# A one-core diffusion block: handovers between layers issued from a build-time plan, and token blocks turned in pairs by a product with diag(scale)

## The chip, the cores and the metric

The kernel runs on one core of one Trainium2 chip. The metric is the device time of one execution in microseconds (us). The engines are named as in the profile: PE is the matrix engine (PEld its weight loads), DVE the vector engine, ACT the scalar engine, POOL the GpSimd engine, SP the engine that issues most DMAs. Each engine runs its own instructions in the order in which they stand in its queue; a wait for another engine is a semaphore.

## The reference, cut to what matters

The program is a two-layer backbone on 512 latent tokens and 256 context tokens of width 1024. Each layer has a token mixer (layer 0 retention, layer 1 HGRN2) and a ConvGLU channel mixer, so there are four sub-layers. Between two sub-layers stands the same piece of arithmetic, and the change is made there:

```python
def rms_norm(x, g):
    y = xf * lax.rsqrt(jnp.mean(xf * xf, -1, keepdims=True) + NORM_EPS)
    return (y * g.astype(jnp.float32)).astype(x.dtype)
...
        h_l = h_l + g1_l * rms_norm(y_l, norm_g[i, 1])
        u_l = rms_norm(h_l, norm_g[i, 2]) * (1.0 + sc2_l) + sh2_l
        h_l = h_l + g2_l * rms_norm(conv_ffn(u_l, ...), norm_g[i, 3])
```

A sub-layer's output y is normalised over the 1024 features of each token, scaled and added to the stream h; h is normalised again and modulated, which gives the next sub-layer's input u. Everything is float32.

## The kernel before

**Arithmetic of the products.** Float32 operands are split into a high and a low part (`split`: an ACT copy makes the high part, a DVE or POOL subtraction the low one), and a product is three matmuls on the parts (`mm3`). Matmuls on operands that were not split, plain float32, are few; each appears in the trace as two rows of PE. A transpose through PE appears as one.

**A handover.** There are four: `m0` after retention and `e0` after the first ConvGLU, on 768 tokens (6 blocks of 128), `m1` after HGRN2 and `e1` after the last ConvGLU, on 512 tokens (4 blocks). In each, `tail` runs the last quarter of the output projection: per block b and half c of the 1024 columns, 12 matmuls into one PSUM bank named `tl`. The order is block by block, the last two blocks interleaved. In the first banks (two, in `m1` four) the last three matmuls are held back. There are six banks of the kind `mm`, which `tl` and `ld` share, and two small ones, used for turned blocks.

**One block after its two banks** (`handover`, generator `block`): DVE adds the bank to y (L375), ACT squares it with a running sum (L376), twice; DVE adds the sums (L377); `rstd` takes ACT for the root (L98) and three short DVE steps (L99 to L101); DVE scales y (L379) and adds it to h (L380); POOL sends h to DRAM (L385); ACT squares h (L386); `rstd` again; ACT writes h times the factor (L389). Then the block is turned from tokens x features to features x tokens: eight transposes on PE against an identity (L396) into two small banks, eight ACT instructions of 128 columns that scale and shift (L399), and the split into the four tiles of u (L56, L57). In `e1` there is no next sub-layer, and SP sends h out (L382).

**After the tail** the next sub-layer's first weights (`lead`, two sets of 256 columns, `fl` or `hl`) are split, the first set's low part on POOL, and `lead` runs their products, 24 matmuls of 256 tokens each into banks named `ld`: per pair of blocks four pieces in `m0`, four or two in `e0`, four in `m1`. A pair must be turned before its pieces run. The turns of the later blocks stand between these pieces (`hooks`).

**What sets the order.** PE's order is written out by hand: each turn stands where `next(gens[b])` is called. The orders of DVE, ACT, POOL and SP come from the framework's scheduler at build time.

Of the kernel before, what the change touches and what calls it, by code (L numbers as in the profile page):

```python
# [15 lines left out]
P = 128  # L16
D = 1024
NF = 8
# [11 lines left out]
LATENT = BOTH[:2]  # L30


class Net:
# [61 lines left out]

    def rstd(self, r, w, ssum, n):
        nc = self.nc
        nc.scalar.activation(r, ssum, AF.Abs_reciprocal_sqrt, bias=self.eps, scale=1.0 / n)  # L98
        nc.vector.tensor_tensor(w, r, r, ALU.mult)  # L99
        nc.vector.scalar_tensor_tensor(w, ssum, n * EPS, w, ALU.add, ALU.mult)  # L100
        nc.vector.scalar_tensor_tensor(r, w, -3.0 * n, r, ALU.add, ALU.mult)  # L101
        return r
# [246 lines left out]
    def handover(self, nm, y, hsrc, gain, mods, u, hdst, nb, big, tmp):  # L349
# [7 lines left out]
        small = lambda n, w: self.cp.tile([P, w], F32, tag=f"sm{w}", name=f"{n}{nm}", bufs=6)  # L357

        def load():
            rows = hsrc.rearrange("(b p) d -> p b d", p=P)  # L360
            for j, x in enumerate(hx):
                n = min(3, nb - 3 * j)
                nc.sync.dma_start(x[:, :n], rows[:, 3 * j : 3 * j + n])
            for v in range(g.shape[1]):
                nc.scalar.dma_start(g[:, v], self.gains[gain][v : v + 1].broadcast_to([P, D]))

        def block(b):
            ts, v = slice(b * P, b * P + P), int(b >= 4)
            yb, hb = y[b // per][:, b % per], hx[b // 3][:, b % 3]
            ss = small(f"ss{b}", 4)  # L370
            r = small(f"r{b}", 2)
            for c in range(2):
                cs = slice(c * 512, c * 512 + 512)
                ps = yield
                nc.vector.tensor_tensor(yb[:, cs], ps, yb[:, cs], ALU.add)  # L375
                nc.scalar.activation(tmp(f"sq{nm}{b}{c}"), yb[:, cs], AF.Square, accum_out=ss[:, c : c + 1])  # L376
            nc.vector.tensor_tensor(ss[:, 2:3], ss[:, 0:1], ss[:, 1:2], ALU.add)  # L377
            ry = self.rstd(r[:, 0:1], r[:, 1:2], ss[:, 2:3], D)
            nc.vector.scalar_tensor_tensor(yb, yb, ry, g[:, v], ALU.mult, ALU.mult)  # L379
            nc.vector.tensor_tensor(hb, hb, yb, ALU.add)  # L380
# [8 lines left out]
            nc.scalar.activation(yb, hb, AF.Copy, scale=rh)  # L389
            yield "z"  # L390
            A, B = mods()
            z = yb.rearrange("p (f c) -> p f c", c=P)
            for j in range(2):
                ps = self.sml(f"tr{nm}{b}{j}")
                for f in range(4):
                    nc.tensor.transpose(ps[:, f * P : f * P + P], z[:, 4 * j + f], self.ident)  # L396
                for f in range(4):
                    k = 4 * j + f
                    nc.scalar.activation(z[:, k], ps[:, f * P : f * P + P], AF.Identity,  # L399
                                         scale=A[:, k, v : v + 1], bias=B[:, k, v : v + 1])  # L400
# [24 lines left out]
    def tail(self, w, x, y, nb, mk, nxt, mid=None):  # L425
        load, gens = mk(nb)
        load()
        for g in gens:
            next(g)

        def part(b, c, kr, ps):
            for k in kr:
                xh, xl = (z[:, b * P : b * P + P] for z in x(k))
                for z, (l, r) in enumerate(((xh, w[c][0]), (xh, w[c][1]), (xl, w[c][0]))):
                    self.nc.tensor.matmul(ps, l, r[:, k], start=(k == 0 and z == 0), stop=(k == 3 and z == 2))  # L435
            if kr[-1] == 3:
                gens[b].send(ps)
# [3 lines left out]
        pss = [self.acc(f"tl{self.uid()}") for _ in range(n0)]  # L441
        for e, ps in zip(order, pss):
            part(*e, range(3), ps)
        if mid is not None:
            self.filler(mid)
        for e, ps in zip(order, pss):
            part(*e, range(3, 4), ps)
        done = 0
        for n, (b, c) in enumerate(order[n0:], n0):
            part(b, c, range(4), self.acc(f"tl{self.uid()}"))  # L450
            if nxt and n >= 6 and n % 2 == 0 and done < nb - 3:
                next(gens[done])
                done += 1
        if not nxt:
            return None
        load, ctx = nxt[0]()
        ws = [z() for z in load]
        turn = lambda b: lambda: next(gens[b])
        if nb == 6:
            hooks = {(0, 0): turn(3), (0, 2): turn(4), (1, 0): turn(5)}  # L460
        else:
            turn(1)()
            hooks = {(0, 0): turn(2), (0, 1): turn(3)}
        return self.lead(ws, ctx, nxt[1](), BOTH if nb == 6 else LATENT, hooks)

# [4 lines left out]
    def lead(self, ws, ctx, u, chunks, hooks):  # L470
        pl = [self.acc(f"ld{self.uid()}") for _ in range(4)]
        pc = [None] * 4
        self.lead_ps = pl, pc
        for z in range(2):
            if ctx[z]:
                bank = self.acc(f"ld{self.uid()}")
                pc[2 * z], pc[2 * z + 1] = bank[:, :TC], bank[:, TC : 2 * TC]
        for ci, (t0, v) in enumerate(chunks):
            for j in range(4):
                if v and pc[j] is None:  # L480
                    continue
# [3 lines left out]
                cs = slice(t0, t0 + W)  # L485
                self.mm3([(o, cs)], [(wh[:, k, ms], wl[:, k, ms], *self.uhl(u, k)) for k in range(NF)])
                if (ci, j) in hooks:
                    hooks[ci, j]()
        return [[(pl[j], LAT)] + ([(pc[j], CTX)] if pc[j] is not None else []) for j in range(4)]

    def first(self, u, big, tmp, extra, epi):
# [94 lines left out]
        self.lead(ws, (True, True), u, BOTH, hooks)  # L586
# [284 lines left out]
    def ffn_lead(self, i):  # L871
        wu = self.t["ffn_w_up"][i].rearrange("(k p) n -> p k n", p=P)

        def load(c):
            return self.weights(wu[:, :, c : c + 256], NF, 256, f"fl{i}{c}", None if c else self.nc.gpsimd)

        return [lambda: load(0), lambda: load(FT * P)], (i == 0, i == 0)
# [437 lines left out]
```

## Time and profile before

| what | value |
|---|---|
| time, median of 3 runs (lowest to highest) | 2200.57 us (2200.57 to 2201.64) |
| the profiled execution's own time | 2201.44 us |
| its span in the profile | 2199.7 us |
| mean granted PE clock | 0.985 of full speed |
| instructions | 30760 |
| HBM read and written | 200.90 MB and 15.34 MB |

The span runs from the first to the last instruction of the trace. Within it the handovers begin at 687.2 (`m0`), 1274.1 (`e0`), 1776.4 (`m1`) and 2167.3 us (`e1`), each counted from its first `tl` matmul. A row of a timeline has a start, a duration, the engine, the line of the kernel, the operation, the tiles out<-in, their shape and a count; in brackets stands how long the engine was idle before it and what ended that. The durations of PE rows overlap, since matmuls are pipelined: what a matmul takes of PE is read from one start to the next.

### The profile page before, as it was taken

The numbers are of one execution on the slowest core, as the hardware profiler recorded it, in microseconds if no ns is written. First come the engines' busy times: TensorE is split into PE (matmuls) and PEld (weight loads), VectorE is DVE, ScalarE is ACT, GpSimd is POOL, SyncE is SP. The second block draws the span as 40 slices with busy tenths as digits, with TensorE's granted clock in tenths as the row PEclk, the third lists the DMA queues.
The fourth block names the chain that finished last, engine by engine and source line by source line (L and its number), as shares of the span: only waits on it lengthen the run. The fifth ranks groups of instructions, "written<-read, shape, count | busy, mean of one in ns | idle before, by whom it ended". The sixth has DMA issues, their size and how long they took to land. (4 is left out here: it accounts for less than half of the span.)

```text
span 2199.7 us, 30760 instructions
## 1 busy us (share of the span) xinstructions
PE 2113.7 (96%) x12288; PEld 1779.3 (81%) x12288; DVE 1340.3 (61%) x2500; ACT 864.3 (39%) x1695; POOL 323.0 (15%) x395
## 2 busy tenths in 40 slices
PE   7999999999899899999999999999999879999998
PEld 5888888888788788788888878888888658888886
DVE  6867565663613567477577566777777754434445
ACT  5543333423524633322132176434443445333323
POOL 4622040210100100000000013333333320000000
PEclk9999999999999999999999999999999999999999
DMA  8113313233123233333333422111111242232232
GB/s 293 51 65 98 111 51 125 78 125 125 39 88 132 69 116 106 112 110 126 124 98 133 174 92 90 59 39 58 39 58 39 77 164 101 93 115 83 92 109 109
DMA packets 186030, 218.21 MB, mean 99 GB/s; under 512 B 6048, under 2 KB 157600, under 8 KB 185120
## 3 DMA queue, kind: packets, MB, share of 16 engines
q1 hardware_dynamic: 179856, 198.90, 27.3%
q0 software_dynamic: 2736, 13.11, 1.6%
q10 hardware_dynamic: 3296, 4.26, 0.6%
q8 instruction: 96, 1.57, 0.3%
q14 instruction: 46, 0.38, 0.1%
HBM read 200.90 MB, written 15.34 MB: 98 GB/s over the span
## 5 line engine op out<-in xcount | busy, mean ns | idle before, releaser
L84 PE MATMUL f<-um,hua 128*128 128x512 f32 (+1 forms) x960 | 258.2, 356 | 0.0
L84 PE MATMUL f<-um,huv 128*128 128x512 f32 (+1 forms) x960 | 255.9, 354 | 0.0
L221 DVE SCALAR_TENSOR_TENSOR rows<-rada,sc,rows 128x256 f32<-128x256 f32 x504 | 231.5, 484 | 5.4
L937 PE MATMUL f<-hd,gt 128*128 128x512 f32 x720 | 228.2, 396 | 0.0
L84 PEld LDWEIGHTS f<-um,hua 128*128 128x128 f32 x960 | 169.6, 189 | 29.3 <-issue 4.0
L84 PE MATMUL hp<-ue,hhw 128*128 128x512 f32 (+1 forms) x672 | 192.0, 373 | 0.0
L84 PEld LDWEIGHTS f<-um,huv 128*128 128x128 f32 x960 | 170.0, 189 | 25.3
L84 PE MATMUL f<-um,lua 128*128 128x512 f32 (+1 forms) x480 | 170.1, 354 | 0.0
L84 PE MATMUL f<-um,luv 128*128 128x512 f32 (+1 forms) x480 | 169.7, 354 | 0.0
L937 PEld LDWEIGHTS f<-hd,gt 128*128 128x128 f32 x720 | 134.9, 187 | 33.6 <-issue 0.8
L937 PE MATMUL f<-ld,gt 128*128 128x512 f32 x360 | 142.2, 395 | 0.0
L84 PEld LDWEIGHTS hp<-ue,hhw 128*128 128x128 f32 x672 | 111.9, 189 | 17.8 <-issue 1.4
L684 PE MATMUL v<-hv,ua 128*128 128x512 f32 x384 | 120.5, 390 | 0.0
L84 PE MATMUL hp<-ue,lhw 128*128 128x512 f32 (+1 forms) x336 | 120.0, 357 | 0.0
L84 PEld LDWEIGHTS f<-um,lua 128*128 128x128 f32 x480 | 90.7, 189 | 13.0
L84 PEld LDWEIGHTS f<-um,luv 128*128 128x128 f32 x480 | 90.7, 189 | 12.6
L909 DVE TENSOR_TENSOR c<-f,c 128x512 f32<-128x512 f32 (+1 forms) x60 | 36.1, 601 | 102.8 <-PE f L84 102.8
L860 PE MATMUL wo<-hwo,ogr 128*128 128x512 f32 x288 | 89.4, 391 | 1.9 <-ACT ogr L56 1.6
L896 ACT ACTIVATE c<-f,c_conv_b,c_conv_w 128x512 f32<-128x512 f32 (+1 forms) x60 | 42.2, 704 | 119.2 <-PE f L84 114.5
L385 POOL DMA_DIRECT2D h_dram<-hxe x6 | 3.2, 539 | 566.9 <-DVE yf L375 541.5
L57 DVE TENSOR_TENSOR lua<-rua,hua 128x512 fp32r<-128x512 f32 x80 | 50.5, 685 | 57.4 <-ACT hua L56 57.2
L56 ACT ACTIVATE hua<-rua 128x512 fp32r<-128x512 f32 x80 | 44.2, 620 | 103.6 <-DMA rua<-ffn_w_up 51.9
(487 smaller groups left out, 4922.0 us busy)
## 6 DMA issues: line engine op xcount, KB each, us to landing
rada<-ada_w SPq DMA_DIRECT2D x48, 1024.0 KB
rua<-ffn_w_up SPq DMA_DIRECT2D x20, 1024.0 KB
ruv<-ffn_w_up SPq DMA_DIRECT2D x20, 1024.0 KB
rd<-ffn_w_down SPq DMA_DIRECT2D x24, 768.0 KB
rhw<-hg_w_in SPq DMA_DIRECT2D x32, 512.0 KB
rv<-ret_w_in SPq DMA_DIRECT2D x8, 1024.0 KB
rg<-ret_w_in SPq DMA_DIRECT2D x8, 1024.0 KB
rqk<-ret_w_in SPq DMA_DIRECT2D x6, 1024.0 KB
```

Of the source, the lines that this page charges most:

```text
L56: self.nc.scalar.activation(hi, raw, AF.Copy)
L57: (eng or self.nc.vector).tensor_tensor(lo, raw, hi.bitcast(F32), ALU.subtract)
L84: nc.tensor.matmul(o, a, b[:, s], start=(i == 0), stop=(i == n - 1))
L221: nc.vector.scalar_tensor_tensor(rows[:, v], raw[:, k], a, rows[:, v], ALU.mult, ALU.add)
L385: nc.gpsimd.dma_start(hdst[ts], hb)
L684: nc.tensor.matmul(ps, a, b, start=(c == 0 and k == 0 and z == 0), stop=(c == 1 and k == 3 and z == 2))
L860: nc.tensor.matmul(ps, l, r[:, k], start=(h == 0 and k == 0 and z == 0), stop=(h == 2 and k == 3 and z == 2))
L896: nc.scalar.activation(c[:, s], ps, AF.Identity, bias=cb[:, i, mt : mt + 1], scale=w(1))
L909: nc.vector.tensor_tensor(c[:, s], ps, c[:, s], ALU.mult)
L937: nc.tensor.matmul(ps, l, r[:, k], start=(k1 + k == 0 and z == 0), stop=(k1 + k == nt - 1 and z == 2))
```

## The change

Three things change in the four handovers; the sub-layers between them keep their code.

1. **A plan orders the handover.** Each step (a bank's 12 matmuls, an addition, a square, a root, a split, a turn, a piece of `lead`) is entered with its engine, a cost in us written in the code, the steps that it needs and a rank. `Plan.run` steps through time with these costs: whenever an engine is free, it emits the ready step of lowest rank there. The order so found is kept on PE, ACT and DVE.
2. **A block is turned by a product.** The pass that wrote h times the factor (L389) goes. Instead DVE makes a 128x128 tile, the identity times the factor of each token (`diag`), and PE multiplies a 128x128 piece of h with it, which turns and scales at once. Two blocks are turned together: a small bank takes two groups of 128 features by 256 tokens, so that a scale-and-shift on ACT covers 256 columns instead of 128. There are as many products (128 in all) as there were transposes; they are plain float32.
3. **Splits and output.** The splits of `lead`'s first weights are plan steps, and their low parts are all on DVE, none on POOL. In `e1` a block's last two DVE steps and its output are done in halves of 512 columns. The line that issues the output picks the queue by `c` when the plan emits it, after the loop over `c` has ended.

```diff
+    def run(self):
+        free = {"PE": 0.0, "ACT": 0.0, "DVE": 0.0, "SP": 0.0}
+        left = list(self.steps)
+        now = 0.0
+        while left:
+            ready = lambda s: max([d.end + 0.1 + s.slack for d in s.deps], default=0.0)
+            known = [s for s in left if all(d.end is not None for d in s.deps)]
+            for eng in free:
+                can = [s for s in known if s.eng == eng and ready(s) <= now and free[eng] <= now]
+                if can:
+                    s = min(can, key=lambda s: s.rank)
+                    s.emit()
+                    s.end = free[eng] = now + s.cost
+                    left.remove(s)
+                    known.remove(s)
+            known = [s for s in left if all(d.end is not None for d in s.deps)]
+            nxt = [max(ready(s), free[s.eng]) for s in known]
+            if left:
+                now = max(now, min(nxt))
...
+        def norms(b, tails):
+            ts, v, pr = slice(b * P, b * P + P), int(b >= 4), b // 2
+            ss, r, q, dg = {}, {}, {}, {}
+            add = self.plan.add
+            half = lambda c: slice(c * 512, c * 512 + 512)
+
+            def evac(c):
+                if not c:
+                    ss[0] = small(f"ss{b}", 4)
+                nc.vector.tensor_tensor(yb(b)[:, half(c)], tails[c].ps, yb(b)[:, half(c)], ALU.add)
+
+            def square(c):
+                nc.scalar.activation(tmp(f"sq{nm}{b}{c}"), yb(b)[:, half(c)], AF.Square, accum_out=ss[0][:, c : c + 1])
...
+            sq = []
             for c in range(2):
-                cs = slice(c * 512, c * 512 + 512)
-                ps = yield
-                nc.vector.tensor_tensor(yb[:, cs], ps, yb[:, cs], ALU.add)
-                nc.scalar.activation(tmp(f"sq{nm}{b}{c}"), yb[:, cs], AF.Square, accum_out=ss[:, c : c + 1])
-            nc.vector.tensor_tensor(ss[:, 2:3], ss[:, 0:1], ss[:, 1:2], ALU.add)
-            ry = self.rstd(r[:, 0:1], r[:, 1:2], ss[:, 2:3], D)
-            nc.vector.scalar_tensor_tensor(yb, yb, ry, g[:, v], ALU.mult, ALU.mult)
-            nc.vector.tensor_tensor(hb, hb, yb, ALU.add)
+                e = add("DVE", 0.67, [tails[c]], (pr, 0), lambda c=c: evac(c))
+                tails[c].freed = e
+                sq.append(add("ACT", 0.75, [e], (pr, 1), lambda c=c: square(c)))
+            n = add("DVE", 0.16, sq, (-1,), lambda: nc.vector.tensor_tensor(ss[0][:, 2:3], ss[0][:, 0:1], ss[0][:, 1:2],
+                                                                            ALU.add))
+            n = add("ACT", 0.28, [n], (-1,), lambda: start(r, ss[0][:, 2:3]))
+            n = add("DVE", 0.55, [n], (-1,), lambda: self.newton(r[0], ss[0][:, 2:3]))
             if u is None:
-                nc.sync.dma_start(hdst[ts], hb)
-                yield "end"
-                return
-            nc.gpsimd.dma_start(hdst[ts], hb)
-            nc.scalar.activation(yb, hb, AF.Square, accum_out=ss[:, 3:4])
-            r2 = small(f"q{b}", 2)
-            rh = self.rstd(r2[:, 0:1], r2[:, 1:2], ss[:, 3:4], D)
-            nc.scalar.activation(yb, hb, AF.Copy, scale=rh)
-            yield "z"
-            A, B = mods()
-            z = yb.rearrange("p (f c) -> p f c", c=P)
-            for j in range(2):
-                ps = self.sml(f"tr{nm}{b}{j}")
-                for f in range(4):
-                    nc.tensor.transpose(ps[:, f * P : f * P + P], z[:, 4 * j + f], self.ident)
-                for f in range(4):
-                    k = 4 * j + f
-                    nc.scalar.activation(z[:, k], ps[:, f * P : f * P + P], AF.Identity,
-                                         scale=A[:, k, v : v + 1], bias=B[:, k, v : v + 1])
-                self.split(u[j][:, :, ts], u[2 + j][:, :, ts], z[:, 4 * j : 4 * j + 4])
-            yield "u"
-
-        return load, [block(b) for b in range(nb)]
+                for c in range(2):
+                    cs = half(c)
+                    n = add("DVE", 1.35, [n], (pr, 2), lambda cs=cs: (
+                        nc.vector.scalar_tensor_tensor(yb(b)[:, cs], yb(b)[:, cs], r[0][:, 0:1], g[:, v, cs],
+                                                       ALU.mult, ALU.mult),
+                        nc.vector.tensor_tensor(hb(b)[:, cs], hb(b)[:, cs], yb(b)[:, cs], ALU.add),
+                        (nc.sync, nc.scalar)[c].dma_start(hdst[ts, cs], hb(b)[:, cs])))
+                return None
+            n = add("DVE", 1.28, [n], (pr, 2), lambda: nc.vector.scalar_tensor_tensor(
+                yb(b), yb(b), r[0][:, 0:1], g[:, v], ALU.mult, ALU.mult))
+            n = add("DVE", 1.23, [n], (pr, 2), lambda: (
+                nc.vector.tensor_tensor(hb(b), hb(b), yb(b), ALU.add), nc.gpsimd.dma_start(hdst[ts], hb(b))))
+            n = add("ACT", 1.23, [n], (pr, 3), lambda: nc.scalar.activation(yb(b), hb(b), AF.Square,
+                                                                           accum_out=ss[0][:, 3:4]))
+            n = add("ACT", 0.28, [n], (-1,), lambda: start(q, ss[0][:, 3:4]))
+            n = add("DVE", 0.55, [n], (-1,), lambda: self.newton(q[0], ss[0][:, 3:4]))
+
+            def diag():
+                dg[0] = self.cp.tile([P, P], F32, tag="diag", name=f"dg{nm}{b}", bufs=4)
+                nc.vector.tensor_scalar(dg[0], self.ident, q[0][:, 0:1], None, ALU.mult)
+
+            n = add("DVE", 0.25, [n], (-1,), diag)
+            return n, dg
+        def turn(pr, ready):
+            add, v, cs = self.plan.add, int(pr == 2), slice(pr * W, pr * W + W)
+            done = []
+            for j in range(4):
+                ps = {}
+
+                def cross(j=j, ps=ps):
+                    ps[0] = self.sml(f"tr{nm}{pr}{j}").rearrange("p (f t) -> p f t", f=2)
+                    for f in range(2):
+                        for z, (_, dg) in enumerate(ready):
+                            k = 2 * j + f
+                            nc.tensor.matmul(ps[0][:, f, z * P : z * P + P], hb(2 * pr + z)[:, k * P : k * P + P], dg[0],
+                                             start=True, stop=True)
+
+                x = yb(2 * pr + j // 2).rearrange("p (f t) -> p f t", f=4)[:, j % 2 * 2 : j % 2 * 2 + 2]
+                hi, lo = (u[z + j // 2][:, j % 2 * 2 : j % 2 * 2 + 2, cs] for z in (0, 2))
+
+                def mod(j=j, ps=ps, x=x):
+                    for f in range(2):
+                        k = 2 * j + f
+                        nc.scalar.activation(x[:, f], ps[0][:, f], AF.Identity, scale=A[:, k, v : v + 1],
+                                             bias=B[:, k, v : v + 1])
+
+                prev = self.cross[-2:][:1] if len(self.cross) > 1 else []
+                t = add("PE", 0.45, [n for n, _ in ready] + prev, (0,), cross, 1.0)
+                m = add("ACT", 0.95, [t], (pr, 4), mod)
+                self.cross.append(m)
+                e = add("ACT", 0.62, [m], (pr, 5), lambda hi=hi, x=x: nc.scalar.activation(hi, x, AF.Copy))
+                done.append(add("DVE", 0.67, [e], (pr, 6), lambda hi=hi, lo=lo, x=x: nc.vector.tensor_tensor(
+                    lo, x, hi.bitcast(F32), ALU.subtract)))
+            return done
...
+        for n, (b, c) in enumerate(order):
+            st = add("PE", 2.73 if n >= n0 else 2.05, [], (1, n + (n >= n0) * 20), None)
+            st.ps = None
+            begin(st, b, c, range(4) if n >= n0 else range(3))
+            parts.append(st)
+        before = [] if mid is None else [add("PE", 0.5, [], (1, 18), lambda: self.filler(mid))]
+        last = list(parts)
+        for n, (b, c) in enumerate(order[:n0]):
+            st = add("PE", 0.68, [parts[n]], (1, 19, n), None)
+
+            def rest(n=n, b=b, c=c):
+                part(parts[n], b, c, range(3, 4))
+                last[n].ps = parts[n].ps
+
+            st.emit = rest
+            last[n] = st
+        by = {e: last[n] for n, e in enumerate(order)}
+        ready = [norms(b, [by[b, c] for c in range(2)]) for b in range(nb)]
+        for n in range(6, len(order)):
+            parts[n].deps.append(last[n - 6].freed)
+        outs = None
+        if nxt:
+            outs = self.lead(*nxt[0](), nxt[1](), BOTH if nb == 6 else LATENT,
+                             [turn(p, ready[2 * p : 2 * p + 2]) for p in range(nb // 2)],
+                             [by[nb - 1, c] for c in range(2)], [p.freed for p in last[-6:]], before)
+        with self.tc.manual_schedule(engines={mybir.EngineType.Activation, mybir.EngineType.DVE}):
+            self.plan.run()
+        return outs and outs()
...
+                e = add("ACT", 0.6, [freed[z], got], (-1 if z == 0 else 1, 9), hi)
+                need[z].append(add("DVE", 0.67, [e], (-1 if z == 0 else 1, 9), lambda ks=ks, raw=raw, hl=hl: (
+                    nc.vector.tensor_tensor(hl[1][:, ks], raw[0][:, ks], hl[0][:, ks].bitcast(F32), ALU.subtract))))
...
+                    add("PE", 2.88, us[ci] + need[j // 2] + banks[:4], (2, ci, j), lambda ci=ci, t0=t0, v=v, j=j:
+                        piece(ci, t0, v, j), 0.2)
```

What this does to the order shows at three places.

PE in `m0`, where the first turned block stands. In the names, `tl` is a bank of the tail, `trm` a small bank, `hwot` and `lwot` the projection's weights, `c_ident` the identity, `dgm` a diagonal tile, `hxm` the stream h and `yr` the scaled copy. Before:

```order
L435 MATMUL tl_5801<-hwot_5615,og_3_4749 128x512
L435 MATMUL tl_5801<-lwot_5616,og_3_4749 128x512
L435 MATMUL tl_5801<-hwot_5615,og_3_4750 128x512
L396 MATMUL trm_5819<-c_ident,yr_5083 128x128 x4
L396 MATMUL trm_5830<-c_ident,yr_5083 128x128 x4
L435 MATMUL tl_5841<-hwot_5627,og_3_4749 128x512
```

Now:

```order
L528 MATMUL tl_5823<-hwot_5615,og_3_4749 128x512
L528 MATMUL tl_5823<-lwot_5616,og_3_4749 128x512
L528 MATMUL tl_5823<-hwot_5615,og_3_4750 128x512
L475 MATMUL trm_5843<-dgm_5768,hxm_5641 128x128
L475 MATMUL trm_5843<-dgm_5837,hxm_5641 128x128
```

`tl_5801` is the seventh bank, `tl_5823` the ninth: the first turn has moved from behind 84 matmuls of the tail to behind 108, and takes blocks 0 and 1 together. In `m1` all 96 matmuls of the tail now stand ahead of the first turn, where there were 84.

DVE in `m1`, between the first block's factor and the second block's (`yh` is y, `ss` the sums, `r` and `q` the factors of y and of h, `lfl` the low part of the next weights). Before:

```order
L99 TENSOR_TENSOR q0m_15481<-q0m_15481 128x1
L99 TENSOR_TENSOR r1m_15401<-r1m_15401 128x1
L100 SCALAR_TENSOR_TENSOR q0m_15481<-ss0m_15398,q0m_15481 128x1
L100 SCALAR_TENSOR_TENSOR r1m_15401<-ss1m_15400,r1m_15401 128x1
L101 SCALAR_TENSOR_TENSOR q0m_15481<-q0m_15481 128x1
L101 SCALAR_TENSOR_TENSOR r1m_15401<-r1m_15401 128x1
L377 TENSOR_TENSOR ss2m_15402<-ss2m_15402 128x1
L379 SCALAR_TENSOR_TENSOR yh_14964<-yh_14964,r1m_15401,hxm_15394 128x1024
L380 TENSOR_TENSOR hxm_15393<-hxm_15393,yh_14964 128x1024
```

Now:

```order
L448 SCALAR_TENSOR_TENSOR yh_14934<-yh_14934,r1m_15492,hxm_15364 128x1024
L142 TENSOR_TENSOR q0m_15517<-q0m_15517 128x1
L143 SCALAR_TENSOR_TENSOR q0m_15517<-ss0m_15436,q0m_15517 128x1
L144 SCALAR_TENSOR_TENSOR q0m_15517<-q0m_15517 128x1
L589 TENSOR_TENSOR lfl_15515<-rfl_15429,hfl_15514 128x512
L459 TENSOR_SCALAR dgm_15539<-c_ident,q0m_15517 128x128
L589 TENSOR_TENSOR lfl_15515<-rfl_15429,hfl_15514 128x512 x3
L451 TENSOR_TENSOR hxm_15363<-hxm_15363,yh_14934 128x1024
L421 TENSOR_TENSOR yh_14935<-tl_15500,yh_14935 128x512
L421 TENSOR_TENSOR yh_14935<-tl_15476,yh_14935 128x512
L421 TENSOR_TENSOR yh_14935<-tl_15525,yh_14935 128x512
L589 TENSOR_TENSOR lfl_15549<-rfl_15431,hfl_15548 128x512
```

Four subtractions of `lfl` now stand between block 1's scaling and its addition to h, and a fifth, of the second set, ahead of its second factor.

ACT at the end of `e1` (`sqe` are squares, `r2e` and `r3e` the factors of the last two blocks, `out` the result). Before:

```order
L376 ACTIVATE sqe_18126,ss3e_18014<-yf_16392 128x512
L376 ACTIVATE sqe_18142,ss2e_18012<-yf_16392 128x512
L98 ACTIVATE r2e_18013<-ss2e_18012,eps 128x1
L376 ACTIVATE sqe_18166,ss3e_18014<-yf_16392 128x512
L98 ACTIVATE r3e_18015<-ss3e_18014,eps 128x1
```

Now:

```order
L424 ACTIVATE sqe_18106,ss3e_18101<-yf_16353 128x512
L424 ACTIVATE sqe_18122,ss2e_18076<-yf_16353 128x512
L428 ACTIVATE r2e_18125<-ss2e_18076,eps 128x1
L446 DMA out<-hxe_17964 128x512
L424 ACTIVATE sqe_18134,ss3e_18101<-yf_16353 128x512
L446 DMA out<-hxe_17964 128x512
L428 ACTIVATE r3e_18140<-ss3e_18101,eps 128x1
L446 DMA out<-hxe_17965 128x512 x2
```

All eight output transfers stand in ACT's queue, none in SP's, and the two of block 2 stand ahead of the last square and the last root of block 3.

More of the change, by code (lines that the diff above doesn't have):

```diff
@@ L30, with __init__, add @@
 LATENT = BOTH[:2]
+class Step:
+    def __init__(self, eng, cost, deps, rank, emit, slack):
+        self.eng, self.cost, self.deps, self.rank, self.emit, self.slack = eng, cost, deps, rank, emit, slack
+        self.end = None
+class Plan:
+    def __init__(self):
+        self.steps = []
+    def add(self, eng, cost, deps, rank, emit, slack=0.0):
+        self.steps.append(Step(eng, cost, list(deps), rank, emit, slack))
+        return self.steps[-1]
+    def run(self):
[17 more added lines that the diff above has]
+                now = max(now, min(nxt))
 class Net:
@@ L356, in handover @@
             g = big([P, 3, D], F32, "gr" + nm)[:, 0:2]
[L357 to L365, printed above, removed]
@@ L404, in handover @@
-        return load, [block(b) for b in range(nb)]
+        small = lambda n, w: self.cp.tile([P, w], F32, tag=f"sm{w}", name=f"{n}{nm}", bufs=12)
+        rows = hsrc.rearrange("(b p) d -> p b d", p=P)
+        for j, x in enumerate(hx):
+            n = min(3, nb - 3 * j)
+            nc.sync.dma_start(x[:, :n], rows[:, 3 * j : 3 * j + n])
+        for v in range(g.shape[1]):
+            nc.scalar.dma_start(g[:, v], self.gains[gain][v : v + 1].broadcast_to([P, D]))
+        yb = lambda b: y[b // per][:, b % per]
@@ L406, in to @@
+        return norms, turn
     @staticmethod
@@ L425, in tail, with part @@
     def tail(self, w, x, y, nb, mk, nxt, mid=None):
[L426 to L431, printed above, removed]
+        self.plan, self.cross = Plan(), []
+        add = self.plan.add
+        norms, turn = mk(nb)
+        def part(step, b, c, kr):
+            if step.ps is None:
+                step.ps = self.acc(f"tl{self.uid()}")
             for k in kr:
@@ L440, in tail @@
         n0 = 2 if mid is None else 4
[L441 to L464, printed above, removed]
+        parts = []
+        def begin(st, b, c, kr):
+            st.emit = lambda: part(st, b, c, kr)
@@ L468, in uid, with lead, hi, piece @@
         return self.n_uid
[L470 to L477, printed above, removed]
+    def lead(self, specs, ctx, u, chunks, us, freed, banks, before):
+        add, nc = self.plan.add, self.nc
+        wt, need, pl, pc = [], [], [], [None] * 4
+        for z, (srcs, name) in enumerate(specs):
+            raw, hl = [], []
+            got = add("SP", 0.1, before, (0,), lambda raw=raw, srcs=srcs, name=name: raw.append(
+                self.wraw(srcs, NF, 256, name)))
+            wt.append(hl)
+            need.append([])
+            for k in range(0, NF, 2):
+                ks = slice(k, k + 2)
+                def hi(ks=ks, raw=raw, hl=hl, name=name):
+                    if not hl:
+                        hl.extend(self.wp.tile([P, NF, 256], F32R, tag=t, name=t[0] + name, bufs=2) for t in ("hi", "lo"))
+                    nc.scalar.activation(hl[0][:, ks], raw[0][:, ks], AF.Copy)
+                e = add("ACT", 0.6, [freed[z], got], (-1 if z == 0 else 1, 9), hi)
+                need[z].append(add("DVE", 0.67, [e], (-1 if z == 0 else 1, 9), lambda ks=ks, raw=raw, hl=hl: (
+                    nc.vector.tensor_tensor(hl[1][:, ks], raw[0][:, ks], hl[0][:, ks].bitcast(F32), ALU.subtract))))
+        def piece(ci, t0, v, j):
+            if not pl:
+                pl.extend(self.acc(f"ld{self.uid()}") for _ in range(4))
+                for z in range(2):
+                    if ctx[z]:
+                        bank = self.acc(f"ld{self.uid()}")
+                        pc[2 * z], pc[2 * z + 1] = bank[:, :TC], bank[:, TC : 2 * TC]
+            wh, wl = wt[j // 2]
+            ms = slice(j % 2 * P, j % 2 * P + P)
+            self.mm3([(pc[j] if v else pl[j][:, t0 : t0 + W], slice(t0, t0 + W))],
+                     [(wh[:, k, ms], wl[:, k, ms], *self.uhl(u, k)) for k in range(NF)])
@@ L585, in first @@
         }
-        self.lead(ws, (True, True), u, BOTH, hooks)
+        self.lead_in(ws, u, hooks)
         each(self.lead_ps[1])
```

51 lines of the change are left out of this document (29 added, 22 removed).

## The prediction

> **What bounds the kernel now.** I read the page's busy shares first, then who PE waits for, then the four handovers as stretches, then the granted clock inside them, and last the timelines around single waits.
>
> ```profile
> PE 2113.7 (96%) x12288; PEld 1779.3 (81%) x12288; DVE 1340.3 (61%) x2500; ACT 864.3 (39%) x1695; POOL 323.0 (15%) x395
> ```
>
> PE is busy for 2113.7 of 2199.7 us, so work that PE alone does is paid in full, and at most 86.0 us is idle PE time. The waits of PE (columns: us in total, times, longest) say how much of that lies in handovers:
>
> ```profile
> PE trm L396 <- ACT yh L389: 12.0, 3, 5.6
> PE trm L396 <- ACT yr L389: 9.0, 3, 4.0
> PE tre L396 <- ACT yf L389: 7.1, 4, 3.1
> PE ld L84 <- ACT um L56: 2.7, 1, 2.7
> ```
>
> 12.0 + 9.0 + 7.1 + 2.7 = 30.8 us: PE stands before a turn until ACT has written the scaled block (L389), once before `lead`'s products. The stretches of `m0`, `e0`, `m1` (first `tl` matmul to the end of `lead`) and of the time after the last matmul:
>
> ```profile
> 687.20:773.70 86.50, 77.50 (x482) 70.46 (x481) 49.65 (x97) 61.17 (x138) 10.70 (x10) 0.94 0.31 107
> 1274.10:1352.60 78.50, 71.38 (x433) 63.37 (x433) 48.97 (x96) 61.63 (x141) 11.93 (x11) 0.96 0.26 87
> 1776.40:1846.90 70.50, 55.64 (x339) 48.89 (x338) 37.38 (x70) 43.16 (x96) 8.38 (x9) 0.90 0.36 128
> 2189.70:2199.70 10.00, 0.00 (x0) 0.00 (x0) 6.04 (x9) 1.02 (x3) 0.00 (x0) 0.60 0.26 105
> ```
>
> Columns: length, busy time of PE, PEld, DVE, ACT, POOL, PE clock, DMA. In no handover are DVE (50, 49, 37 us) or ACT (61, 62, 43) near the length; it is the serial chain of a block that comes late. The clock is below 1 there, and the profile shows where: behind the waits, in pieces of the clock's grid.
>
> ```profile
> 724.20:727.60 3.40, 3.40 (x10) 0.54 0.00 0
> 734.50:741.20 6.70, 6.17 (x30) 0.52 0.58 185
> 1311.30:1314.70 3.40, 3.40 (x10) 0.54 0.00 0
> 1328.40:1331.70 3.30, 3.10 (x15) 0.53 0.09 27
> 1802.80:1806.20 3.40, 3.27 (x12) 0.54 0.98 344
> 1813.10:1823.30 10.20, 7.17 (x31) 0.51 0.44 155
> ```
>
> The second number is PE's busy time at half clock: 9.6 us in `m0`, 6.5 in `e0`, 10.4 in `m1`. Half of each is lost. At full clock PE's work is therefore 77.5 - 4.8 = 72.7 us in `m0`, 71.4 - 3.2 = 68.2 in `e0` and 55.6 - 5.2 = 50.4 in `m1`. The rest, 13.8, 10.3 and 20.1 us, is what an order without waits could win.
>
> **What the product costs.** Start to start, a transpose and a plain float32 product of the same 128x128x128 size:
>
> ```profile
> 706.29 1.03 PE L396 MATMUL trm<-c_ident,yr 128*128 128x128 f32 x8
> 707.08 0.48 PE L435 MATMUL tl<-hwot,og 128*128 128x512 f32 x1
> ...
> 1766.83 1.16 PE L1119 MATMUL hc<-hv,KT 128*128 128x128 f32 x8 [0.66 <-ACT KT L1112]
> 1767.75 0.48 PE L84 MATMUL hwo<-hhwo,hgs 128*128 128x512 f32 x1
> ```
>
> Eight transposes take 0.79 us, 0.099 each. The eight rows of `hc` are four products (two rows each) and take 0.92, 0.23 each. A turn thus costs 0.13 us more: 48 x 0.13 = 6.3 us in `m0` and in `e0`, 32 x 0.13 = 4.2 in `m1`, 16.8 in all, on the engine that bounds. This is what the change pays. Its lower bound is nothing more than a transpose (0), its upper the unpipelined row pair, about 0.39.
>
> [...]
>
> **m0 and e0: does PE still wait?** The first turn needs both blocks' factors, so block 1's chain decides. PE now has 108 matmuls ahead of it.
>
> ```profile
> 687.23 0.39 PE L435 MATMUL tl<-hwot,og 128*128 128x512 f32 x1
> ...
> 706.06 0.39 PE L435 MATMUL tl<-hwot,og 128*128 128x512 f32 x1
> ...
> 707.86 0.15 DVE L101 SCALAR_TENSOR_TENSOR q1m<-q1m 128x1 f32<-128x1 f32 x1
> ```
>
> The first 84 take 18.83 us for 83 steps, 0.227 each; 108 take 24.5, so PE arrives at 711.7. Before the change block 1's second factor was ready at 708.0, 20.8 us after the start, with DVE's other blocks already in between. Two diagonal tiles come on top; a DVE instruction on 128x128 took 0.28:
>
> ```profile
> L1124 DVE COPY s<-hc x16: 276/280/292, 1401.3 to 1770.7; 128x128 f32<-128x128 f32 x16
> L399 ACT ACTIVATE yr<-trm,mod,mv0A x48: 438/470/512, 707.5 to 755.7; 128x128 f32<-128x128 f32 x48
> L896 ACT ACTIVATE c<-ld,c_conv_b,c_conv_w x6: 548/766/778, 760.3 to 1843.7; 128x512 f32<-128x512 f32 x4, 128x256 f32<-128x256 f32 x2
> L57 POOL TENSOR_TENSOR lfl<-rfl,hfl x4: 1258/1278/1311, 1796.3 to 1800.0; 128x512 fp32r<-128x512 f32 x4
> ```
>
> Ready at about 708.6, so some 3 us of slack (bounds of the unseen diagonal step: 0.15 as the shortest DVE rows, 0.7 as a 512-wide one; the slack covers both). On ACT a block loses the L389 pass, 1.1 us, and the scale-and-shift falls from eight times 0.47 to four times 0.55 per block (the 256-wide form): 3.8 to 2.2 us. On DVE come four `lfl` subtractions of 0.6, while POOL's four of 1.28 go; next to those DVE rows stretched (a 0.16 us step took 2.55, shown below). The later pairs stand behind 24 `tl` matmuls, and behind two pieces of `lead` each (48 matmuls, 5.8 us), with eight or more turns' worth of ACT time free. So I cost both handovers at PE's work alone: `m0` 72.7 + 6.3 = 79.0, a gain of 7.5; `e0` 68.2 + 6.3 = 74.5, a gain of 4.0. What hides the chain is the tail and the two pieces; if that cover is gone, the wait returns with the half clock behind it.
>
> **m1: a wait stays.** All 96 tail matmuls now stand ahead of the first turn, and nothing of `lead` can be put there.
>
> ```profile
> 1787.13 2.77 DVE L375 TENSOR_TENSOR yh<-tl,yh 128x512 f32<-128x512 f32 x4 [4.27 <-PE tl L435]
> 1791.26 0.16 DVE L101 SCALAR_TENSOR_TENSOR r0m<-r0m 128x1 f32<-128x1 f32 x1
> 1798.76 2.55 DVE L99 TENSOR_TENSOR q0m<-q0m 128x1 f32<-128x1 f32 x1 [0.70 <-ACT q0m L98]
> ```
>
> PE ends the tail at 1776.4 + 96 x 0.227 + 1.0 (an `ada` product between) = 1799.2. The first four additions and block 0's first factor come as before, 1791.4. From there DVE's new row order gives block 0's scaling and addition (1.28 + 1.23), three steps of 0.19 for r1, an addition 0.6, block 1's scaling 1.2, q0 0.57, one `lfl` and the tile 0.8, three `lfl` 1.8, block 1's addition 1.2: 9.3 us, 1800.7. ACT squares it (1.16) and takes the root (0.3), DVE three steps and the tile: about 1804. PE waits 4.5 us, then for small banks and for the first parts of u some 3.5 in four short pieces (a pair of scale-and-shifts 1.1, a split 0.6 + 0.7, against 0.9 us of products): 8 in all, bounds 5 and 11. A wait of 4 us was followed by 3.4 to 6.8 us at half clock before, so 1.7 to 3.4 us more, 2.5 taken. `m1` comes to 50.4 + 4.2 + 8 + 2.5 = 65.1, a gain of 5.4. The wait of 2.55 above, beside POOL's `lfl`, goes; it is in the 20.1.
>
> **e1: the end gets longer.** After the last matmul (2189.7) there is nothing beside the chain.
>
> ```profile
> 2189.72 0.69 DVE L375 TENSOR_TENSOR yf<-tl,yf 128x512 f32<-128x512 f32 x1 [0.18 <-PE tl L435]
> 2190.51 0.63 ACT L376 ACTIVATE sqe<-yf 128x512 f32<-128x512 f32 x1 [1.55 <-DVE yf L375]
> ...
> 2191.71 0.29 ACT L98 ACTIVATE r3e<-ss3e,eps 128x1 f32<-128x1 f32 x1 [0.48 <-DVE ss3e L377]
> ...
> 2194.68 1.22 DVE L380 TENSOR_TENSOR hxe<-hxe,yf 128x1024 f32<-128x1024 f32 x1
> ...
> 1780.71 0.75 DVE L1142 SCALAR_TENSOR_TENSOR hog<-qg,c_hg_gn,rhg 128x512 f32<-128x512 f32 x1
> 1775.29 0.36 ACTq L365 DMA_DIRECT2D hxm<-gain  x1
> ```
>
> Before, the square ran beside block 2's scaling, and DVE ended 6.2 us after PE. Now a transfer that waits for DVE stands ahead of the square on ACT, a second one ahead of the root, and DVE itself stands before block 3's sum: addition 0.6, half of block 2 (0.75 + 0.69), issue 0.36, square and its sum 0.75, sum 0.16, other half 1.44, issue 0.36, root 0.29, three steps 0.57, block 3 in halves 2.8: 8.8 us, 2.6 later. The last transfer is half as large; 512 KB at the 400 GB/s seen there is 1.3 us, so 0.6 comes back. I take +2.0, bounds +1 and +3.
>
> **The sum.** -7.5 - 4.0 - 5.4 + 2.0 = -14.9 against the profiled execution's 2201.44, which is 0.87 above the median: 2186.5 there, 2185.7 as a median. The steps between handovers keep their order. I forecast **2185 us**, the small-product price of 0.22 that single pairs of rows show rounding it down.
>
> **The rivals.** *The chains are a fifth slower than their rows* (handoffs between engines add up, the plan's costs were too hopeful): then the slack of 3 us in `m0` and `e0` is gone, each waits some 3 us, `m1` 3 more, and half clock takes 2 to 3 again: 2185 + 11 = 2196. For it: plan costs of 0.45 for a turn step that takes 0.9 show that the plan does not know its engines. Against it: the order is fixed, and an underrated PE step leaves DVE and ACT more time, not less. *The wait in m1 goes too*, because additions of later blocks and `lfl` fit better than my row sum: 2185 - 8 = 2177; ACT's queue order speaks against it. [...] *The change does not do what it says*: the scheduler could reorder DVE and ACT after the plan; the printed order shows the plan's, so I give this no share of its own.
>
> **How the numbers follow.** Forecast 0.63 (2180 to 2191), slower chains 0.19 (2191 to 2200), no wait in `m1` 0.12 (2172 to 2180), four passes 0.06 (2200 to 2210). The range leaves out the fourth, the far half of the second's upper end and the edge of the third: 2176 to 2196. A measurement of this kernel can tell 0.2%, 4.4 us, from no change. Faster than 2196.2: the forecast, the third and two thirds of the second, 0.88; within 0.2%: the rest of the second and a little of the fourth, 0.07; slower 0.05.
>
> **What would show it.** In the profile after: 12416 rows of PE; in the stretches of `m0` and `e0` no wait above 0.5 us before a turn, a clock of 1.0, and lengths of 78 to 80 and 73 to 76; in `m1` one wait of 4 to 5 us before the second product of the first turn, put down to the diagonal tile on DVE, and a piece at half clock; start to start 0.9 us for a turn of four products; after the last matmul some 12 us with ACT's transfers between its squares. A turn of 1.6 us, or waits before the first turn of `m0`, would prove the forecast wrong.

## The result and the profile after

The changed kernel takes 2182.91 us (median of 4 runs, 2181.15 to 2183.92) against 2200.57 us, a ratio of 0.9917 with a 95% interval of 0.9905 to 0.9929: 17.7 us faster, where 15.6 had been forecast. Its profiled execution spans 2180.4 us, 19.3 less than that of before. All stretches below are from such profiled executions.

The busy shares of the changed kernel, the first row of its page:

```profile
PE 2117.5 (97%) x12416; PEld 1787.0 (82%) x12416; DVE 1344.1 (62%) x2536; ACT 832.3 (38%) x1615; POOL 304.3 (14%) x383
```

PE has the 128 extra rows of the products, yet its busy time has grown by only 3.8 us, since fewer rows run at half clock (the mean granted clock is 0.991, where it was 0.985). The waits of PE that belong to handovers (us in total, times, longest) are few:

```profile
PE trm L475 <- DVE dgm L459: 3.8, 1, 3.8
...
PE ld L121 <- DVE um L492: 1.0, 1, 1.0
...
PE ld L121 <- ACT um L491: 0.6, 1, 0.6
```

30.8 us have become 5.4, and all of it lies in `m1`. The stretches of `m0`, `e0`, `m1` (from the first `tl` matmul to the first matmul after `lead`) and the end, with the columns of before (length, busy time of PE, PEld, DVE, ACT, POOL, PE clock, DMA):

```profile
688.31:766.27 77.96, 77.96 (x529) 72.26 (x528) 50.07 (x107) 49.27 (x108) 3.26 (x6) 1.00 0.33 118
1266.75:1339.92 73.17, 73.17 (x481) 66.58 (x481) 48.32 (x104) 48.56 (x108) 3.22 (x7) 1.00 0.30 99
1762.23:1825.66 63.43, 58.04 (x370) 52.15 (x369) 38.33 (x78) 35.14 (x76) 3.37 (x5) 0.95 0.41 142
2168.50:2180.40 11.90, 0.00 (x0) 0.00 (x0) 6.83 (x13) 1.02 (x3) 0.00 (x0) 0.66 0.23 88
```

In the first two rows the length is PE's busy time and the clock is 1.00: PE alone sets these stretches. `m1` keeps 5.4 us of idle time and two pieces of 3.4 us at a granted clock of 0.50 (from 1790.0 and from 1800.2). The account, measured from the same marks in both kernels:

| stretch | before, us | after, us | difference | forecast |
|---|---|---|---|---|
| `m0` | 86.43 | 77.96 | -8.5 | -7.5 |
| `e0` | 78.50 | 73.17 | -5.3 | -4.0 |
| `m1` | 70.47 | 63.43 | -7.0 | -5.4 |
| after the last matmul | 10.0 | 11.9 | +1.9 | +2.0 |
| all between them | 1954.3 | 1953.9 | -0.4 | 0 |

The last row is within what these stretches vary by, so nothing is read from it: the stretch before `m0` lasted between 686.35 and 688.61 us in the profiles of the nine kernels seen here, and that between `e0` and `m1` between 422.3 and 424.2.

The place where `m0` hands over, on DVE and PE (the diagonal tile of block 1, the first turn, the next matmul of the tail):

```profile
710.93 0.28 DVE L459 TENSOR_SCALAR dgm<-c_ident,q1m 128x128 f32<-128x128 f32 x1
712.84 1.95 PE L475 MATMUL trm<-dgm,hxm 128*128 128x128 f32 x16
714.54 0.48 PE L528 MATMUL tl<-hwot,og 128*128 128x512 f32 x1
```

The tile is ready at 711.21 and PE comes at 712.84: 1.6 us of slack (time by which the tile is early), and no wait. In `m1` the same step waits, and the timeline shows what came late:

```profile
1782.73 1.89 DVE L589 TENSOR_TENSOR lfl<-rfl,hfl 128x512 fp32r<-128x512 f32 x3
...
1784.54 1.22 DVE L451 TENSOR_TENSOR hxm<-hxm,yh 128x1024 f32<-128x1024 f32 x1
...
1785.70 0.39 PE L475 MATMUL trm<-dgm,hxm 128*128 128x128 f32 x2
1785.95 1.15 ACT L585 ACTIVATE hfl<-rfl 128x512 fp32r<-128x512 f32 x2 [2.45 <-issue]
...
1787.01 1.04 ACT L452 ACTIVATE yh<-hxm 128x1024 f32<-128x1024 f32 x1
...
1789.56 0.28 DVE L459 TENSOR_SCALAR dgm<-c_ident,q1m 128x128 f32<-128x128 f32 x1
...
1789.89 0.52 PE L475 MATMUL trm<-dgm,hxm 128*128 128x128 f32 x1 [3.80 <-DVE dgm L459]
```

Block 1's addition starts at 1784.54, straight behind subtractions of `lfl`. It ends at 1785.76, but ACT squares its result only at 1787.01: in front of the square stand two high parts of the second weight set, and these, which the plan lets begin when the tail's last bank is done (`freed`), start at 1785.95, as PE leaves the tail. So in each of two queues a step that PE does not need yet stands ahead of the one that it needs.

After the last matmul ACT's transfers (ACTq is its queue) stand where the forecast saw them:

```profile
2168.50 0.69 DVE L421 TENSOR_TENSOR yf<-tl,yf 128x512 f32<-128x512 f32 x1 [0.18 <-PE tl L528]
...
2170.61 0.34 ACTq L446 DMA_DIRECT2D out<-hxe  x1
2171.00 0.63 ACT L424 ACTIVATE sqe<-yf 128x512 f32<-128x512 f32 x1 [3.26 <-DVE hxe L445]
...
2171.75 0.16 DVE L435 TENSOR_TENSOR ss3e<-ss3e 128x1 f32<-128x1 f32 x1 [1.17 <-ACT sqe L424]
...
2173.33 0.34 ACTq L446 DMA_DIRECT2D out<-hxe  x1
2173.72 0.30 ACT L428 ACTIVATE r3e<-ss3e,eps 128x1 f32<-128x1 f32 x1 [2.00 <-DVE hxe L445]
```

The last square could have started when its block's addition ended, at 2169.2, and the root when the sum was there, at 2171.9. Each starts 1.8 us late, right behind a transfer that waited for DVE.

### The profile page after: what moved, and what is told of

It reads as the page before. It is cut to its first block, busy times and chain, and to the rows that moved or that the text cites. A ratio compares the mean times of both kernels' runs of the same rounds, so it can differ in the third digit from the quotient of the medians.

```text
span 2180.4 us, 30973 instructions
## 1 busy us (share of the span) xinstructions
PE 2117.5 (97%) x12416; PEld 1787.0 (82%) x12416; DVE 1344.1 (62%) x2536; ACT 832.3 (38%) x1615; POOL 304.3 (14%) x383
## 5 line engine op out<-in xcount | busy, mean ns | idle before, releaser
L819 PEld LDWEIGHTS v<-hv,ua 128*128 128x128 f32 x384 | 72.1, 188 | 15.4 <-issue 0.6
```

The costliest lines, as they stand in the source:

```text
L819: nc.tensor.matmul(ps, a, b, start=(c == 0 and k == 0 and z == 0), stop=(c == 1 and k == 3 and z == 2))
```

## The experiments

The first two kernels part the diagonal products from the rest of the change. In the diffs `[...]`, `...` and a bare line of dots stand for what is left out.

**The plan with the old turn.** Everything of the change stays but the product: the planned order, two blocks turned together, the low parts on DVE, the halves in `e1`. ACT writes the scaled copy again and PE transposes it against the identity; the scaled-and-shifted result goes to a scratch tile, because the copy is still being read.

```diff
+            def scale():
+                nc.scalar.activation(yb(b), hb(b), AF.Copy, scale=q[0][:, 0:1])
+
+            if True:
+                n = add("ACT", 1.13, [n], (pr, 3), scale)
+                return n, None
...
-                            nc.tensor.matmul(ps[0][...], hb(2 * pr + z)[...], dg[0], start=True, stop=True)
...
+                                nc.tensor.transpose(o, yb(2 * pr + z)[:, ks], self.ident)
```

> The plan stays, the second part of the change is undone: ACT writes the scaled copy of each block again (1.1 us each, 16 blocks), PE turns it by transposes against the identity, 256 tokens a pair as now. Theory A (PE bounds m0 and e0, the plan alone hides the chain): 128 turns times 0.224 - 0.099 us, 16.0 us less PE work; the first turn of a handover slips by 1.1 - 0.3 = 0.8 us, less than the 1.6 us by which the diagonal tile was early in m0. m0 72, e0 67.2, m1 60 us, total 2169 (2166 to 2172). Theory B (the pass that was taken out is what makes the handovers free of waits, because ACT is the next engine): waits before turns come back in m0 and e0, 3 us or more in each, and total is 2175 to 2186. PE rows 12288 in both.

Measured: 2172.94 us, ratio 0.9874 (0.9861 to 0.9888) to the kernel before. Its three handovers, and the waits of PE in `m1` (first) and `e0` that are longest:

```profile
688.38:763.26 74.88, 73.19 (x481) 66.83 (x480) 48.87 (x100) 55.00 (x113) 3.25 (x6) 1.00 0.36 125
1263.74:1333.89 70.15, 68.46 (x433) 61.17 (x433) 47.22 (x98) 54.98 (x114) 3.20 (x7) 1.00 0.31 102
1756.33:1816.51 60.18, 53.28 (x339) 46.84 (x338) 37.16 (x73) 39.02 (x80) 3.37 (x5) 0.94 0.44 150
```

```profile
PE trm L483 <- ACT yh L462: 4.9, 1, 4.9
...
PE ld L121 <- DVE ue L504: 0.9, 2, 0.6
PE ld L121 <- ACT ue L503: 0.8, 1, 0.8
```

Between the two theories and nearer to A: 1.7 us of waits come back in `m0` and in `e0` (length less PE's busy time), before `lead`'s products and not before turns, and `m1` is 3.3 us shorter though its longest wait is 4.9. Block 1's scaled copy and the first turn of `m0` stand here:

```profile
710.04 1.15 ACT L462 ACTIVATE yr<-hxm,q1m 128x1024 f32<-128x1024 f32 x1 [0.28 <-DVE q1m L144]
...
715.61 1.03 PE L483 MATMUL trm<-c_ident,yr 128*128 128x128 f32 x8
```

The copy is ready at 711.2, no later than the diagonal tile was, but the plan, which reckons 1.13 us for the pass and 0.25 for the tile, has put the first turn one bank later: 27.2 us after the start where it was 24.5. The turned blocks come later, and `lead`'s products wait for them. **Without the product the change is worth 27.7 us, 10.0 more than as made.**

**The products without the plan.** PE's order, POOL's work and the blocks turned one by one are those of before; DVE and ACT are again ordered by the framework's scheduler, and their order differs in places.

```diff
-            nc.scalar.activation(yb, hb, AF.Copy, scale=rh)
+            dg = self.cp.tile([P, P], F32, tag="diag", name=f"dg{nm}{b}", bufs=4)
+            nc.vector.tensor_scalar(dg, self.ident, rh, None, ALU.mult)
...
-                    nc.tensor.transpose(ps[:, f * P : f * P + P], z[:, 4 * j + f], self.ident)
+                    nc.tensor.matmul(ps[:, f * P : f * P + P], hb[:, k * P : k * P + P], dg, start=True, stop=True)
```

> The kernel before with the second part of the change alone: a diagonal tile on DVE in place of the scaling pass on ACT, products in place of transposes, block by block, the old order. Theory A (the plan is what takes the waits away, the products only cost): 16.0 us more PE work, each of the eleven waits of 30.8 us shorter by 1.1 - 0.3 = 0.8 us: +16 - 9 = 2208 (2204 to 2212). Theory B (the product's longer PE time stands where PE waited, and the shorter chain does the rest): PE is busy where it stood, the half clock behind the waits goes with them, and the total falls: 2190 to 2198.

Measured: 2201.08 us against 2200.67, ratio 1.0001 (0.9991 to 1.0010): no change. The handovers:

```profile
686.35:770.47 84.12, 80.19 (x529) 73.97 (x528) 52.56 (x103) 54.66 (x132) 8.31 (x10) 0.98 0.31 109
1270.91:1348.83 77.92, 73.88 (x482) 66.77 (x482) 52.24 (x102) 55.42 (x135) 9.56 (x11) 1.00 0.27 89
1772.98:1845.79 72.81, 60.86 (x370) 54.15 (x369) 38.29 (x74) 39.03 (x92) 8.37 (x9) 0.91 0.35 124
```

Neither theory's total, because both effects are there. In `m0` PE's idle time falls from 9.0 to 3.9 us while its busy time rises from 77.5 to 80.2 (5.5 us of products, less half-clock time that went with the waits), and 2.3 us are gained. In `m1`, where the waits stay long, 2.3 us are lost. So the product buys back waits with PE time, at about the same rate. On top of the rest of the change, which has removed most waits already, there is little left to buy and the price is paid: the two effects, -27.7 and 0, do not add up to the -17.7 of the change.

**What these two kernels do not part.** The plan came together with the move of `lead`'s low parts from POOL to DVE. In the two kernels with PE's old order POOL's subtractions run beside slow rows of DVE. In `m0` of the kernel before, and then of this one:

```profile
719.57 7.46 POOL L57 TENSOR_TENSOR lfl<-rfl,hfl 128x512 fp32r<-128x512 f32 x4 [8.03 <-ACT hfl L56]
...
721.37 2.28 DVE L379 SCALAR_TENSOR_TENSOR yr<-yr,r3m,grm 128x1024 f32<-128x1024 f32 x1
```

```profile
718.68 5.89 DVE L57 TENSOR_TENSOR um<-yr,um 128x512 fp32r<-128x512 f32 x1
...
719.00 5.01 POOL L57 TENSOR_TENSOR lfl<-rfl,hfl 128x512 fp32r<-128x512 f32 x4
...
725.20 0.63 ACT L376 ACTIVATE sqm<-yr 128x512 f32<-128x512 f32 x1 [2.99 <-DVE yr L375]
```

The same rows of DVE take 1.28 and 0.68 us elsewhere in `m0`. They stand in the chains of block 3 (before) and block 4 (here), the blocks before whose turns PE then waits longest, 4.00 and 3.05 us; in `e0` here the longest wait before a turn is 3.05 us as well. With the plan POOL no longer makes these low parts. So part of the 27.7 us may be the move off POOL and not the order; no run makes the one without the other, and the share of each stays open.

**The price of a turn.** The same plan, with transposes in place of products, against a tile with ones on the diagonal that DVE still makes from the factor. The turned blocks of this kernel lack the second normalisation's scale:

```diff
-                nc.vector.tensor_scalar(dg[0], self.ident, q[0][:, 0:1], None, ALU.mult)
+                nc.vector.tensor_scalar(dg[0], self.ident, q[0][:, 0:1], 0.0, ALU.mult, ALU.is_lt)
...
-                            nc.tensor.matmul(ps[0][...], hb(2 * pr + z)[...], dg[0], start=True, stop=True)
+                            nc.tensor.transpose(ps[0][...], hb(2 * pr + z)[...], dg[0])
```

> The changed kernel with each product of a turn replaced by a transpose against a tile that DVE still makes from the second factor (ones on the diagonal instead of the factor): the second normalisation's scale is left out of the turned stream. Waits and order are unchanged, only the price of a turn on PE changes. Theory A (0.224 against 0.099 us a turn, PE the bound in m0 and e0): m0 and e0 6.0 us shorter each, m1 2 to 4, total 2167 to 2169. Theory B (ACT and DVE set the pace as soon as PE is quicker): waits before turns appear and less than half of it comes, total 2175 or more. [...]

Measured: 2169.26 us. The handovers `m0` and `e0`, and eight transposes of `m0` with the next matmul:

```profile
688.55:761.03 72.48, 72.48 (x481) 66.67 (x480) 49.72 (x106) 48.57 (x107) 3.25 (x6) 1.00 0.36 128
1261.49:1329.17 67.68, 67.68 (x433) 61.00 (x433) 48.14 (x104) 48.44 (x108) 3.21 (x7) 1.00 0.32 106
...
713.09 1.04 PE L475 MATMUL trm<-dgm,hxm 128*128 128x128 f32 x8
713.89 0.47 PE L527 MATMUL tl<-hwot,og 128*128 128x512 f32 x1
```

No idle time and full clock in both, and each 5.5 us shorter: 0.114 us a turn. Start to start a transpose takes 0.80 / 8 = 0.100 us; a product, from the sixteen rows of `m0` above, (714.54 - 712.84) / 8 = 0.213. Theory A holds, with 13.7 us in place of 14 to 16. The two lengths are also what PE's own work takes there without products.

**What holds up `m1`.** Two kernels. The first ranks the four low parts on DVE behind block 1's scaling and addition; the second also plans the second set's high parts on ACT later:

```diff
-                need[z].append(add("DVE", 0.67, [e], (-1 if z == 0 else 1, 9), lambda ...
+                need[z].append(add("DVE", 0.67, [e], ((0, 5) if z == 0 else (1, 9)), lambda ...
...
-                e = add("ACT", 0.6, [freed[z], got], (-1 if z == 0 else 1, 9), hi)
+                e = add("ACT", 0.6, [freed[z], got], (-1 if z == 0 else 1, 9), hi, 2.5 * z * (len(chunks) == 2))
```

> The changed kernel with another rank for the four low parts of lead's first weights on DVE: behind block 1's scaling and addition, not ahead of them. Theory A (these four subtractions, 2.4 us, hold up block 1's addition and so the first turn of m1): the wait of 3.8 us before the second product falls under 1.5 us, m1 goes from 63.4 to 60 to 61.5 us, total 2180 to 2181.5. Theory B (ACT's queue holds it: two high parts of the second set, which wait for the end of the tail, stand ahead of block 1's square): the wait stays above 3 us and the total at 2182 to 2184. m0 and e0 keep their lengths within 0.5 us.

> As m1_low, and in m1 the high parts of the second set on ACT are planned 2.5 us later, so that block 1's square stands ahead of them. Theory A (DVE's order was the cause): no more than 0.5 us better than m1_low. Theory B (ACT's order was the cause): the wait of 3.8 us goes only here, m1 60 to 61 us against 63 in m1_low.

Measured: 2180.83 and 2178.01 us. The stretch `m1` of the first, with rows of its timeline, and the stretch of the second:

```profile
1763.26:1823.45 60.19, 56.74 (x371) 50.67 (x369) 39.25 (x79) 35.41 (x76) 3.39 (x5) 0.97 0.42 150
...
1782.93 1.22 DVE L451 TENSOR_TENSOR hxm<-hxm,yh 128x1024 f32<-128x1024 f32 x1
...
1784.44 1.05 ACT L452 ACTIVATE yh<-hxm 128x1024 f32<-128x1024 f32 x1
...
1787.46 1.83 PE L475 MATMUL trm<-dgm,hxm 128*128 128x128 f32 x14 [0.34 <-DVE dgm L459]
...
1791.36 1.90 PE L475 MATMUL trm<-dgm,hxm 128*128 128x128 f32 x11 [2.07 <-ACT yh L484]
```

```profile
1762.17:1821.62 59.45, 55.76 (x371) 49.26 (x369) 39.36 (x79) 35.53 (x76) 3.37 (x5) 1.00 0.43 153
```

Theory A: with the subtractions out of the way block 1's addition stands 2.6 us earlier against the tail's start, its square no longer meets the second set on ACT, the wait of 3.80 falls to 0.34 and `m1` to 60.2. A later wait of 2.07 us takes part of its place: it is for the scale-and-shift, which on ACT now stands behind the second set. In the second kernel PE's idle time is no shorter (3.7 us against 3.45), but it comes in pieces of 1.0 at most, and the clock stays at 1.00: `m1` is 0.7 us shorter, a little more than the 0.5 that theory A allowed. The medians differ by 2.8 us, the two profiled spans by 1.8; of that 0.7 lies in `m1` and 1.2 between `e0` and `m1`, where the kernels are the same.

**The end.** The half is bound in the lambda when the step is recorded:

```diff
-                    n = add("DVE", 1.35, [n], (pr, 2), lambda cs=cs: (
+                    n = add("DVE", 1.35, [n], (pr, 2), lambda cs=cs, c=c: (
```

> The changed kernel with the half bound in the lambda of e1, so that the output transfers alternate between SP's queue and ACT's: ACT no longer stands in front of the last square and the last root. Theory A (two transfers ahead of the square and the root cost the end): the stretch after the last matmul goes from 11.9 to 9.9 us, total 2181. Theory B (halves and DVE's own order cost it): the stretch stays at 11.5 or more. All other stretches stay.

Measured: 2180.83 us, and the stretch after the last matmul:

```profile
2170.30:2181.00 10.70, 0.00 (x0) 0.00 (x0) 6.74 (x13) 1.02 (x3) 0.00 (x0) 0.68 0.26 98
...
2173.89 0.34 ACTq L446 DMA_DIRECT2D out<-hxe  x1
2174.27 0.29 ACT L428 ACTIVATE r3e<-ss3e,eps 128x1 f32<-128x1 f32 x1 [2.44 <-DVE hxe L445]
```

11.9 becomes 10.7, not 9.9: a miss in size. The square is free, but the second half of block 2 is still issued by ACT and still stands ahead of block 3's root, which waits 2.44 us for DVE.

**The best of them together**: the plan with the old turn, both edits of `m1`, and all output transfers in SP's queue (`nc.sync` for both halves).

> The plan with the scaling pass and transposes (as plan_scaled), with both changes of m1_low_high, and with all output transfers of e1 in SP's queue. If the three are independent: m0 74.9 and e0 70.2 as in plan_scaled, m1 60.2 less 2 to 3, the end 12.0 less 1.9 to 2.2 (neither square nor root waits for a transfer): 2172.9 - 4.5 = 2168.4 (2167 to 2170). If ACT, which has the scaling passes again, sets m1's pace, m1 stays within 1 us of 60.2 and the total is 2170 to 2171.

Measured: 2169.33 us (2168.51 to 2170.21), ratio 0.9858 (0.9841 to 0.9874), 13.6 us faster than the change as made. `m1` and the end:

```profile
1755.81:1814.12 58.31, 54.54 (x339) 48.21 (x338) 37.23 (x73) 38.93 (x80) 3.37 (x5) 0.91 0.43 155
2156.90:2166.80 9.90, 0.02 (x1) 0.00 (x0) 6.65 (x13) 1.02 (x3) 0.00 (x0) 0.69 0.28 106
```

The end is at 9.9 us, that of before: the whole +1.9 was transfers in ACT's queue, and the halves cost nothing on balance (DVE ends 0.8 us later than before, and the last, smaller transfer takes 0.9 less). `m1` gives 1.9, a little under the 2 to 3 expected. Waits are not the reason: PE's idle time there falls by 3.1 us, from 6.9 to 3.8, but its busy time grows by 1.3 at a granted clock of 0.91, where it was 0.94. The wait before the turn, for ACT's scaling pass, is still 2.0 us, where it was 4.9. The total lies in the range of the independent sum.

## Why the prediction was right

- **What bounds it, and the time at half clock.** The forecast took 72.7 and 68.2 us as PE's own work at full clock in `m0` and `e0`; the kernel with transposes shows 72.5 and 67.7. Reading half of each half-clock piece as lost was sound.
- **The price of the product.** 0.13 us a turn was taken, 0.114 measured. The term was 6.3 us in `m0` and in `e0`; it is 5.5. The rows of `hc` gave 0.23 for a product, where a longer run of them takes 0.213. No run shows the 0.40 us of "four passes", to which the forecast gave 0.06: a product took 0.213, 2.1 times the 0.100 of a transpose.
- **m0 and e0 without waits.** Right: no idle time. The slack was 1.6 us and not 3, since block 1's tile stands on DVE behind an addition that itself waits for PE's tail. The rival of chains a fifth slower did not come. Even the old scaling pass brings no wait before the first turn, in an order planned for it.
- **m1.** The step was right in place and mechanism, the wait before the second product 3.8 us where 4.5 was summed, and the short pieces behind it 1.6 us in two where 3.5 in four were summed; in all 5.4 instead of 8, the largest error of a term. By the kernel with both edits PE's work there at full clock is about 55.8 us, 1.2 more than taken. The tile came 27.6 us after the start, which is what "about 1804" says, but in part by luck: the sum had DVE's addition 0.8 us too late and did not hold ACT's two high parts, which delay the square by 1.25, and its listed rows give 1803.0, so that up to 1.0 us in it has no row.
- **The end.** +1.9 against +2.0, with the cause as argued: transfers issued by ACT. DVE ended 9.0 us after PE where 8.8 was summed, and the smaller last transfer gave 0.9 back where 0.6 was taken. The last kernel removes the +1.9 whole.
- **What it did not ask.** It called the products what the change pays, and set that against a gain of the whole change. It did not work out the plan without them, which the same rows allowed: the slack of 3 us that it had worked out for `m0` and `e0` would have covered the scaling pass, 0.8 us longer, as well. Right on the sum, it says nothing on which part earns it; the kernels without the product and with it alone show that the product does not. It saw that DVE rows stretch beside POOL's subtractions (2.55 us for a step of 0.16), yet gave their removal no term of its own.

The 4.4 us between the forecast sum (-14.9) and the spans (-19.3) are 1.6 from the product's price and 0.7 from PE's own work in `m0` and `e0`, 1.7 from `m1`, and 0.4 from the stretches between.

## What to carry to other kernels

Two edits against the same wait are measured apart before they are kept together: here the plan, with the low parts moved off POOL, removed most of the waits, and work moved onto the bounding engine to shorten the chain then cost 10 us more than it saved. A planner that takes the first ready step lets a step that nobody needs yet stand ahead of one that PE waits for; look for such steps in the queues of the engines that PE waits on, and for a wait of another engine in front of them. An engine that computes on the last chain should issue no transfer that waits for another engine: in the changed kernel such transfers cost 1.9 us.

## What was not expected of the hardware

A wait of the same length was followed by half clock in one place and not in another. In the kernel with products in the old order PE stands 3.05 us before a turn once in `m0` and once in `e0`:

```profile
739.33 2.89 PE L398 MATMUL trm<-dgm,hxm 128*128 128x128 f32 x14 [3.05 <-DVE dgm L390]
...
1324.68 2.02 PE L398 MATMUL tre<-dge,hxe 128*128 128x128 f32 x16 [3.05 <-DVE dge L390]
```

The turn is sixteen rows in both. To the start of the next matmul they take 2.96 us in `m0` and 1.78 in `e0`; the mean granted clock of the two stretches is 0.98 and 1.00. No run shows what decides between the two. For a forecast of this kernel this means that the half-clock term behind a wait of about 3 us is a chance and not a sum.

DVE was slow beside POOL. In the kernel with the products alone a subtraction of 128x512 on DVE took 5.89 us while POOL ran its four, and 0.68 elsewhere. In the kernel before, an addition of 128x1024 took 2.19 us beside them and 1.22 elsewhere. What causes it was not tested.
